# Attention's value products with the values stationary in column halves, and the mixing factors read back in 3 KB runs

## The chip, the cores and the metric

The kernel runs on one core of a Trainium2 chip. The metric is the time of one execution on the device in microseconds, taken as the median of several. TensorE multiplies (the page calls its matmuls PE and its weight loads PEld), VectorE is DVE, ScalarE is ACT, GpSimd is POOL, and SyncE is SP, which here only issues transfers.

## The reference

One layer of an encoder on 1024 tokens of width 1024. A projection `h @ w_in` feeds a dilated window attention, a gated linear attention and two merge gates; their merge, a norm and an MLP follow. What the change touches is the attention, for four head slots of width 64 and three groups g with dilations 1, 4 and 16:

```python
s = jnp.einsum('brnqhd,brnkhd->brnhqk', qb, kw) * (dh ** -0.5) + bias   # masked to the band
m = jnp.max(s, axis=-1, keepdims=True)
e = jnp.exp(s - m)
den = jnp.sum(e, axis=-1, keepdims=True)
o = jnp.einsum('brnhqk,brnkhd->brnhqd', e, vw) / den
lse = m + log(den)
```

For every token and head slot the three groups' outputs are added with weights proportional to their denominators. So with the numerators num_g = e @ v, the output is the sum over g of f_g num_g, where f_g = exp(m_g - max m) / sum over g of (exp(m_g - max m) den_g): three groups times four heads are twelve factors f for a token.

## The kernel before, in words

**Stage.** The large projections go through `mm3` (L100 to L103), three matmuls of 512 columns in a split float format for each product. They are cut in steps, and attention is cut in 24 tiles of 128 queries, groups 2, 1 and 0 in that order, eight tiles t0 to t7 each. `visit(i)` (one for each of 27 places among the steps) runs the parts of up to four tiles, so that attention's instructions fall between dense matmuls. A scheduler then fixes the order of each engine's instructions when the program is built; on the chip each engine runs its list in order and waits on semaphores.

**A tile.** `load` fetches q and k (POOL queue). `scores` (L803) multiplies in row halves, two heads at a time; VectorE adds the bias and takes the minimum (L809), ScalarE the exponential with its sum (L814); minima and sums lie in `sm`. `turned` transposes e on TensorE (L830) and copies it out as `et` (L837). `values` (L844) multiplies with `et` stationary, 128 by 128, and the 64 columns of a head's values moving, into `av` with the queries on the partitions. Each matmul in plain float shows as two records.

**Mixing.** For groups 2 and 1 numerators and `sm` are copied together into `st` (L854, L855) and stored as rows of 264 floats in `rows` (POOL queue). For group 0 a tile reads back 128 rows of each other group into R (L821), `weigh` (L881 to L884) and `blend` (L889 to L898) form the factors with queries on partitions, multiply the numerators by them and add. Two transposes on TensorE (L872), a copy (L873) and a store by POOL (L874) put the result in `yadr`, head dimension on partitions.

**After it.** `branches` (L963) loads `ygdr` (the other mixer) and `yadr` in pieces of 128x512 through SP into `pre`; ScalarE and VectorE split each in two parts, `yg` and `ya` (L148, L149). The merge multiplies them (`ps<-yg`, `ps<-ya`) and needs gates loaded from `spill` (`gate<-spill`, L1004); the tiles of the gates lie in memory that attention used.

Of the kernel before, what the change touches and what calls it, by code (L numbers as in the profile page):

```python
# [7 lines left out]
F32 = mybir.dt.float32  # L8
# [3 lines left out]
AF = mybir.ActivationFunctionType  # L12
OP = mybir.AluOpType
# [4 lines left out]
S = 1024  # L18
# [9 lines left out]
ORD = (1, 4, 8)  # L28
# [43 lines left out]
def build(tc, io):  # L72
    nc = tc.nc
    V, G, A, T, SP = nc.vector, nc.gpsimd, nc.scalar, nc.tensor, nc.sync
    P = Pools(tc)
    issued = {}
# [7 lines left out]
    avp = P.open("av", bufs=1, space=PSUM)  # L84
    dr = P.open("dram", space=DRAM)

    def load_w(src, shape, raw=None):
        if raw is None:
            raw = wp.tile(shape, F32, tag="raw", bufs=2, name="raw")
            issued["raw"] = SP.dma_start(raw, src)  # L90
        hi = wp.tile(shape, F32R, tag="whi", bufs=4, name="whi")
        A.copy(hi, raw)
        lo = wp.tile(shape, F32R, tag="wlo", bufs=4, name="wlo")
        V.tensor_tensor(lo, raw, hi.bitcast(F32), op=OP.subtract)  # L94
        return hi, lo
# [14 lines left out]
    ygdr = dr.tile([4, 128, S], F32, name="ygdr")  # L110
    sdr = dr.tile([2, 5, 128, 2, 512], F32, name="sdr")
    yadr = dr.tile([2, 128, S], F32, name="yadr")
    rows = dr.tile([2, S, 264], F32, name="rows")
    tdr = dr.tile([12, 128, 512], F32, name="tdr")
    trow = dr.tile([12, 512], F32, name="trow")
    vdr = dr.tile([S, 768], F32, name="vdr")
# [67 lines left out]
    for k in range(KT):  # L184
        n = {0: 1, 1: 1, 2: 2, 4: 2, 6: 2}.get(k)
# [18 lines left out]
    ident = cp.tile([128, 128], F32, name="ident")  # L204
# [12 lines left out]
    tp = trp.tile([128, 512], F32, tag="tr", name="tr")  # L217
# [491 lines left out]
    p0, p1 = projs[:2]  # L709
# [7 lines left out]
    a, b = p0["steps"][1], p0["steps"][4]  # L717
# [15 lines left out]
    ap_ = P.open("att", reuse_waits="tile")  # L733
# [11 lines left out]
    kq_t, kk_t, kv_t = (ring(ap_, [128, 2, n], F32, m, nm) for nm, n, m in (("aq", 128, 3), ("ak", 256, 2), ("av", 256, 3)))  # L745
    e_t, et_t = (ring(ap_, [128, 2, 256], F32, m, nm) for nm, m in (("e", 4), ("et", 3)))
    sm_t, f_t = ring(ap_, [128, 8], F32, 3, "sm"), ring(ap_, [128, 5, 4], F32, 2, "f")
    st_t, R_t = ring(ap_, [128, 264], F32, 2, "st"), ring(ap_, [128, 3, 264], F32, 2, "R")
    sc_t = turns([scp.tile([128, 2, 256], F32, tag="sc", name="sc") for _ in range(2)], 2)
    tr_t = turns([trp.tile([128, 2, 256], F32, tag="tr", name="tr") for _ in range(2)], 2)  # L750
    av = avp.tile([128, 256], F32, tag="av", name="avp")
    yat = ap_.tile([128, 2, 128], F32, name="yat")

    def window(g, t):

        if g == 2:
            return 128, 128, t * 128
        if g == 1:
            return (192, 256)[t % 2], (128, 0)[t % 2], t // 2 * 256
        return 192 if t in (0, 7) else 256, 128 if t == 0 else 64, min(max(128 * t - 64, 0), 832)  # L760

    def att(g, t):

        w, b0, k0 = window(g, t)
        b = {}
# [49 lines left out]
                                                 accum_out=sm[:, 4 + h:5 + h])  # L815

        def turned():
            if g == 0:
                b["R"] = R_t()
                for i in range(2):  # L820
                    G.dma_start(b["R"][:, 1 + i], rows[i, t * 128:t * 128 + 128])  # L821
            b["et"] = []
            nb = len(b["blks"])
            for i in range(2):
                tp, et = (x.rearrange("p a (b n) -> p a b n", n=128) for x in (tr_t(), et_t()))
                b["et"].append(et)
                for pr in range(2):
                    for j, (lo, hi, vv, p0) in enumerate(b["blks"]):
                        with tc.issue_after(issued["small"].ins):
                            T.transpose(tp[0:hi - lo, pr, j], b["e"][i][:, pr, lo:hi], ident)  # L830
                cpy = A.copy if i else V.tensor_copy
                if w == 192 and t < 7:
                    j = 0 if g == 0 else 1
                    cpy(et[0:64, :, j], tp[0:64, :, j])
                    cpy(et[:, :, 1 - j], tp[:, :, 1 - j])
                else:
                    cpy(et[:, :, 0:nb], tp[:, :, 0:nb])  # L837

        def values():
            nb = len(b["blks"])  # L840

            def part(j, h):
                lo, hi, vv, p0 = b["blks"][j]
                return T.matmul(av[:, h * 64:h * 64 + 64], b["et"][h % 2][p0:p0 + vv.shape[0], h // 2, j],  # L844
                                vv[:, h * 64:h * 64 + 64], start=j == h == 0, stop=j == nb - 1,
                                skip_group_check=True)

            with tc.issue_after(part(0, 0).ins):
                for j in range(nb):
                    for h in range(4):  # L850
                        if j or h:
                            issued["small"] = part(j, h)
            st = b["R"][:, 0] if g == 0 else st_t()
            V.tensor_copy(st[:, 0:256], av)  # L854
            V.tensor_copy(st[:, 256:264], b["sm"])  # L855
            if g == 1:
                G.dma_start(rows[0].rearrange("(u j c) w -> c u j w", u=2, c=4)[t // 2, t % 2], st)
            elif g == 2:
                G.dma_start(rows[1].rearrange("(j r) w -> r j w", r=8)[t], st)
            else:  # L860
                b["f"] = weigh(b["R"])

        def mix():
            if g == 0:
                b["o"] = o = st_t()[:, 0:256]
                blend(b["R"], b["f"], o)

        def mixed():
            if g == 0:
                tp = tr_t()  # L870
                for pr in range(2):
                    T.transpose(tp[:, pr, 0:128], b["o"][:, pr * 128:pr * 128 + 128], ident)  # L872
                A.copy(yat, tp[:, :, 0:128])  # L873
                G.dma_start(yadr[:, :, t * 128:t * 128 + 128].rearrange("b p n -> p b n"), yat)  # L874

        return load, scores, turned, values, mixed, mix

    def weigh(R):
        nm = R[:, :, 256:260]
        f = f_t()  # L880
        V.tensor_tensor(f[:, 3], nm[:, 0], nm[:, 1], op=OP.min)  # L881
        V.tensor_tensor(f[:, 3], f[:, 3], nm[:, 2], op=OP.min)
        V.tensor_tensor(f[:, 0:3], f[:, 3:4].to_broadcast([128, 3, 4]), nm, op=OP.subtract)
        A.activation(f[:, 0:3], f[:, 0:3], AF.Exp)  # L884
        return f

    def blend(R, f, o):
        den = R[:, :, 260:264]
        V.tensor_tensor(den, den, f[:, 0:3], op=OP.mult)  # L889
        V.tensor_tensor(f[:, 4], den[:, 0], den[:, 1], op=OP.add)  # L890
        V.tensor_tensor(f[:, 4], f[:, 4], den[:, 2], op=OP.add)
        V.reciprocal(f[:, 4], f[:, 4])
        V.tensor_tensor(f[:, 0:3], f[:, 0:3], f[:, 4:5].to_broadcast([128, 3, 4]), op=OP.mult)
        for g in range(3):
            num = R[:, g, 0:256].rearrange("p (h d) -> p h d", h=4)
            V.tensor_tensor(num, num, f[:, g].unsqueeze(2).to_broadcast([128, 4, 64]), op=OP.mult)
        V.tensor_tensor(R[:, 0, 0:256], R[:, 0, 0:256], R[:, 1, 0:256], op=OP.add)
        V.tensor_tensor(o, R[:, 0, 0:256], R[:, 2, 0:256], op=OP.add)  # L898

    def flat(t):  # L900
        return t.rearrange("p a b -> p (a b)")[:, 0:512]


    gated = ap_.tile([128, 3, 512], F32, tag="strip1", name="gated")
    gating = (turns([flat(e_t()) for _ in range(4)] + [flat(R_t()) for _ in range(2)], 6),
              turns([flat(et_t()) for _ in range(3)] + [gated[:, i] for i in range(3)], 6),
              turns([flat(kv_t()) for _ in range(3)], 3))

    def silu(h, hf):
# [15 lines left out]
        return load, do  # L925

    tiles = [att(g, t) for g in (2, 1, 0) for t in range(8)]

    issued["small"] = issued["pe"]

    def visit(i):

        for n, part in ((i + 1, 0), (i - 2, 3), (i, 1), (i - 1, 2), (i - 2, 5), (i - 3, 4)):
            if 0 <= n < 24:
                tiles[n][part]()


    n0 = len(steps) + 14
    for p in projs[2:]:
        steps += p["steps"]  # L940
    n1 = len(steps) - 7
    units = {}
    for i in range(27):
        units.setdefault(n0 + 1 + i * (n1 - n0) // 27, []).append(lambda i=i: visit(i))
    for i in range(8):

        n = n0 - 18 + i * 3 // 2
# [103 lines left out]
    w = []  # L1051
# [96 lines left out]
    w = [load_w(io["wo"][1, k2], [128, 2, 512]) for k2 in range(4)]  # L1148
# [241 lines left out]
    p0, p1 = pairs[:2]  # L1390
# [87 lines left out]
    R = {}  # L1478
# [326 lines left out]
```

## Time and profile before

| | |
|---|---|
| median of 3 runs | 1380.35 us (1380.32 to 1381.3) |
| the profiled execution | 1383.76 us |
| its span, and TensorE's granted clock | 1382.0 us, 0.997 |
| TensorE busy | 1370.8 us, 99% |
| VectorE, ScalarE, POOL busy | 73%, 46%, 7% |
| attention's tiles on TensorE | from 306 to 574 us |
| values, L844 | 320 records |

The span is what the profiler saw between the first and the last instruction; the execution's own time is 1.76 us longer. A row of the timeline gives start, duration, engine, line, operation, output<-inputs and shapes, and a count where like rows follow one another. Matmuls are pipelined and the end of each is modelled, so the cost of one is read from start to start of its neighbours.

### The profile page before, as it was taken

The numbers are of one execution on the slowest core, as the hardware profiler recorded it, in microseconds if no ns is written. First come the engines' busy times: TensorE is split into PE (matmuls) and PEld (weight loads), VectorE is DVE, ScalarE is ACT, GpSimd is POOL, SyncE is SP. The second block draws the span as 40 slices with busy tenths as digits, with TensorE's granted clock in tenths as the row PEclk, the third lists the DMA queues.
The fourth block names the chain that finished last, engine by engine and source line by source line (L and its number), as shares of the span: only waits on it lengthen the run. The fifth ranks groups of instructions, "written<-read, shape, count | busy, mean of one in ns | idle before, by whom it ended". The sixth has DMA issues, their size and how long they took to land.

```text
span 1382.0 us, 19028 instructions
## 1 busy us (share of the span) xinstructions
PE 1370.8 (99%) x6837; PEld 1153.0 (83%) x6837; DVE 1011.3 (73%) x1748; ACT 630.7 (46%) x1207; POOL 99.1 (7%) x153
## 2 busy tenths in 40 slices
PE   9999999999999999999999999999999999999998
PEld 6989998788888888888888888888888888888886
DVE  6377768677565677666667787878867897786988
ACT  5346645334344344354416655555556433333343
POOL 0000100013222232000001000000000000000002
PEclk9999999999999999999999999999999999999998
DMA  7262326575444443465753565666655965445313
GB/s 247 71 190 87 108 71 225 183 206 176 157 145 159 136 143 127 139 225 191 270 213 141 200 221 191 222 208 217 219 205 157 365 220 167 152 131 160 105 31 122
DMA packets 105907, 238.57 MB, mean 173 GB/s; under 512 B 20101, under 2 KB 28805, under 8 KB 105812
## 3 DMA queue, kind: packets, MB, share of 16 engines
q1 hardware_dynamic: 99220, 218.47, 47.4%
q0 software_dynamic: 6304, 18.49, 4.4%
q8 instruction: 54, 0.88, 0.3%
q10 hardware_dynamic: 288, 0.39, 0.1%
q14 instruction: 41, 0.34, 0.1%
HBM read 160.67 MB, written 77.68 MB: 172 GB/s over the span
## 4 chain that ended last, share of the span: by engine, by line
PE 90%; DVE 3%; DMA 2%; issue 2%; ACT 2%; POOL 0%; SPq 0%; POOLq 0%; ACTq 0%; DVEq 0%
PE ps L101 18%; PE ps L102 18%; PE ps L103 18%; PE mm L101 9%; PE mm L102 9%; PE mm L103 9%; PE avp L844 2%; PE tr L830 1%; PE sc L803 1%; ACT xr L1196 1%; DMA xrh<-in_xT 1%; DMA praw<-in_wfm 1%; PE sc L406 0%; PE tr L376 0%; DMA pwhi<-in_wfm 0%
## 5 line engine op out<-in xcount | busy, mean ns | idle before, releaser
L1177 ACT CAST T<-hp 128x1024 fp32r<-128x1024 f32 x36 | 37.8, 1051 | 107.6 <-PE ps L102 68.1
L102 PE MATMUL mm<-wlo,x 128*128 128x272 f32 (+1 forms) x240 | 74.5, 311 | 0.7 <-DVE wlo L94 0.7
L101 PE MATMUL mm<-whi,x 128*128 128x272 f32 (+1 forms) x240 | 75.0, 313 | 0.0
L103 PE MATMUL mm<-whi,x 128*128 128x272 f32 (+1 forms) x240 | 74.6, 311 | 0.0
L814 ACT ACTIVATE e<-e,sm 128x256 f32<-128x256 f32 (+2 forms) x96 | 43.4, 453 | 51.6 <-DVE sm L809 51.6
L102 PE MATMUL ps<-B,B 128*128 128x512 f32 x160 | 62.2, 389 | 0.0
L103 PE MATMUL ps<-B,B 128*128 128x512 f32 x160 | 62.2, 389 | 0.0
L101 PE MATMUL ps<-B,B 128*128 128x512 f32 x160 | 60.9, 390 | 0.5 <-ACT B L1177 0.5
L101 PE MATMUL ps<-T,T 128*128 128x512 f32 x144 | 56.0, 389 | 0.0
L102 PE MATMUL ps<-B,T 128*128 128x512 f32 x144 | 56.0, 389 | 0.0
L102 PE MATMUL ps<-T,T 128*128 128x512 f32 x144 | 56.0, 389 | 0.0
L103 PE MATMUL ps<-B,T 128*128 128x512 f32 x144 | 56.0, 389 | 0.0
L103 PE MATMUL ps<-T,T 128*128 128x512 f32 x144 | 56.0, 389 | 0.0
L101 PE MATMUL ps<-B,T 128*128 128x512 f32 x144 | 56.0, 389 | 0.0
L1578 DVE TENSOR_TENSOR acc<-ps,acc 128x512 f32<-128x512 f32 x68 | 45.8, 690 | 12.8 <-PE ps L103 12.2
L1178 DVE TENSOR_TENSOR T<-hp,T 128x1024 fp32r<-128x1024 f32 x36 | 44.1, 1224 | 14.1 <-ACT T L1177 14.0
L101 PE MATMUL mm<-x,pwlo 128*128 128x512 f32 x128 | 51.1, 399 | 1.4 <-DVE cu L642 1.4
L642 DVE TENSOR_TENSOR cr<-cu,mm 128x512 f32<-128x512 f32 x44 | 35.2, 800 | 23.3 <-PE mm L103 23.0
L1683 POOL TENSOR_TENSOR mv<-mv,mhalf 128x1 f32<-128x1 f32 x8 | 7.0, 880 | 607.3 <-DVE mv L1682 605.8
L103 PE MATMUL mm<-x,pwlo 128*128 128x512 f32 x128 | 50.0, 391 | 0.0
L102 PE MATMUL mm<-x,pwlo 128*128 128x512 f32 x128 | 50.0, 391 | 0.0
L101 PE MATMUL ps<-T,fraw 128*128 128x512 f32 x128 | 49.6, 390 | 0.4 <-ACT T L1177 0.4
(497 smaller groups left out, 4228.8 us busy)
## 6 DMA issues: line engine op xcount, KB each, us to landing
hdr<-c SPq DMA_DIRECT2D x112, 256.0 KB, 2.5
hp<-hdr SPq DMA_DIRECT2D x56, 512.0 KB, 3.6
spill<-cr SPq DMA_DIRECT2D x64, 256.0 KB, 3.0
praw<-in_wfm SPq DMA_DIRECT2D x16, 512.0 KB, 5.0
pwhi<-in_wfm SPq DMA_DIRECT2D x16, 512.0 KB, 4.6
gate<-spill SPq DMA_DIRECT2D x32, 256.0 KB, 3.7
wa<-in_w SPq DMA_DIRECT2D x16, 512.0 KB, 4.5
wb<-in_w SPq DMA_DIRECT2D x16, 512.0 KB, 6.4
```

Source lines behind the costliest of these rows:

```text
L101: T.matmul(ps, lh, rh, start=first and i == 0, stop=False, skip_group_check=more)
L102: T.matmul(ps, lh, rl, start=False, stop=False, skip_group_check=more)
L103: issued["pe"] = T.matmul(ps, ll, rh, start=False, stop=last and i == n - 1, skip_group_check=more)
L642: issued["add"] = V.tensor_tensor(o, a, b, op=OP.add)
L803: mm = T.matmul(sps[i][:, pr, 0:w], q[ps_, pr], k[ps_, pr, 0:w], start=True, stop=True)
L814: issued["exp"] = A.activation(e, e, AF.Exp, bias=sm[:, h:h + 1], scale=-1.0, accum_out=sm[:, 4 + h:5 + h])
L830: T.transpose(tp[0:hi - lo, pr, j], b["e"][i][:, pr, lo:hi], ident)
L844: return T.matmul(av[:, h * 64:h * 64 + 64], b["et"][h % 2][p0:p0 + vv.shape[0], h // 2, j], vv[:, h * 64:h * 64 + 64], start=j == h == 0, ...
L1177: A.copy(o[:, 0], src)
L1178: V.tensor_tensor(o[:, 1], src, o[:, 0].bitcast(F32), op=OP.subtract)
L1196: A.activation(q[i][:, k], tp[:, k], AF.Identity, bias=cols[:, c + 8:c + 9], scale=cols[:, c:c + 1])
L1578: V.tensor_tensor(m, p, m, op=OP.add)
```

## The change

**Values.** They are now the stationary operand, 64 columns wide, and `et` moves with 128 columns. Heads of even and odd number go to the left and the right half of the array's columns; the output has the head dimension on the partitions (two heads in one column of 128) and the queries as columns, as `yadr` wants it. The transposes of L872 and their copies go.

**Stores.** For groups 2 and 1 numerators go to `numdr` and `sm` alone to `smdr`, both by POOL. `quarter` reads the numerators back for two tiles at a time, by four SP transfers in runs of 256 and 128 B; `stats` reads the sums of all tiles, by POOL, into `s12`.

**Factors.** For group 0 they are formed right behind the scores (`weigh`) and a step later (`shares`), turned from 128x12 to 12x128 by TensorE (`spread`, L901), copied to `fT` by ScalarE, stored in `fdr` by ScalarE's queue, and read back by SP (`loadw`, L909): each half of the partitions gets one run of 3 KB, the same for each partition. This W has the shape of the numerators, so that four kinds of products and two sums on VectorE (L859 to L868) do the mixing, straight into what POOL stores in `yadr`. There is one W and one R.

The core of the diff (left out: the tiles' declarations in DRAM, the removed blend, the removed transposes):

```diff
+    R, W = ap_.tile([128, 2, 2, 256], F32, name="R"), ap_.tile([128, 3, 2, 128], F32, name="W")
+    st_t = turns([R[:, 1, i].rearrange("p (b n) -> p b n", b=2) for i in range(2)], 2)
...
-                return T.matmul(av[:, h * 64:h * 64 + 64], b["et"][h % 2][p0:p0 + vv.shape[0], h // 2, j],
-                                vv[:, h * 64:h * 64 + 64], start=j == h == 0, stop=j == nb - 1,
+                return T.matmul(av[64 * i:64 * i + 64, pr], vv[:, h * 64:h * 64 + 64],
+                                b["et"][i][p0:p0 + vv.shape[0], pr, j], start=j == pr == 0, stop=j == nb - 1,
                                 skip_group_check=True)
...
+            if g:
+                st = st_t()
+                V.tensor_copy(st, av[:, 0:2])
+                G.dma_start(numdr[g - 1, :, :, t * 128:t * 128 + 128].rearrange("b p n -> p b n"), st)
+                return
+            o = V.tensor_tensor(W[:, 0], av[:, 0:2], W[:, 0], op=OP.mult)
+            for i in range(2):
+                c = ORD[i + 1]
+                n = 128 // c
+                num = R[:, i].rearrange("p b (c j) -> p b j c", c=c)[:, :, t % 2 * n:t % 2 * n + n]
+                wn = W[:, i + 1].rearrange("p b (j c) -> p b j c", c=c)
+                for pr in range(2):
+                    with tc.issue_after(o.ins):
+                        o = V.tensor_tensor(wn[:, pr], num[:, pr], wn[:, pr], op=OP.mult)
+                V.tensor_tensor(mixed if i else W[:, 0], W[:, 0], W[:, i + 1], op=OP.add)
+            G.dma_start(yadr[:, :, t * 128:t * 128 + 128].rearrange("b p n -> p b n"), mixed)
...
+        def spread():
             if g == 0:
+                with tc.issue_after(issued["pe"].ins):
+                    issued["small"] = T.transpose(av[0:12, 2], b["f"][:, 0:3].rearrange("p g h -> p (g h)"), ident)
+                A.copy(fT, av[0:12, 2])
+                A.dma_start(fdr[t].rearrange("i r n -> r i n"), fT)
+
+        def loadw():
+            if g == 0:
+                for i in range(2):
+                    one = fdr[t, i:i + 1].rearrange("i r n -> i (r n)")
+                    SP.dma_start(W[64 * i:64 * i + 64].rearrange("p g b n -> p (g b n)"), one.to_broadcast([64, 768]))
...
+    def quarter(n):
+        u, q = n // 2, n % 2
+        for g in (1, 2):
+            c = ORD[g]
+            for pr in range(2):
+                src = numdr[g - 1, pr].rearrange("p (c u q j) -> p u q c j", c=c, u=2, q=2)[:, u, q]
+                dst = R[:, g - 1, pr].rearrange("p (c j) -> p c j", c=c)
+                SP.dma_start(dst, src)
...
-        for n, part in ((i + 1, 0), (i - 2, 3), (i, 1), (i - 1, 2), (i - 2, 5), (i - 3, 4)):
+        for n, part in ((i + 1, 0), (i - 1, 6), (i - 2, 3), (i, 1), (i - 1, 2)):
...
+    for i in range(26):
+        n = n0 + 1 + i * (n1 - n0) // 27
+        units.setdefault(n, []).append(lambda i=i: visit(i))
+        for k, part, later in ((i, 4, 1), (i, 5, 2), (i - 1, 7, 1)):
+            if 0 <= k < 24 and (later == 1 or k > 15):
+                units.setdefault(n + later, []).append(lambda k=k, part=part: tiles[k][part]())
+        if i in (17, 19, 21, 23):
+            units[n + 1].append(lambda i=i: quarter((i - 17) // 2))
```

The order moves where attention ends. On TensorE before, at the last attention work (the numbers behind names are buffers; L101 to L103 are dense matmuls):

```order
L844 MATMUL avp<-av_2253,et_2260 128x64
L872 MATMUL tr<-ident,st_2266 128x128 x2
L101 MATMUL mm<-x_91,pwlo 128x512
...
L103 MATMUL mm<-x_89,pwlo 128x512
L872 MATMUL tr<-ident,st_2267 128x128 x2
L101 MATMUL mm<-x_89,pwlo 128x512
```

And of the change, from the last dense matmul to the first merge products (`et_2262` with `av_2254` is t6, `av_2255` t7):

```order
L103 MATMUL mm<-x_94,px 128x512
L901 MATMUL avp<-ident,f_2267 12x128
L845 MATMUL avp<-et_2262,av_2254 64x128
...
L845 MATMUL avp<-et_2260,av_2254 64x128
L830 MATMUL tr<-ident,e_2258 128x128 x4
L830 MATMUL tr<-ident,e_2259 128x128 x4
L845 MATMUL avp<-et_2261,av_2255 64x128
...
L101 MATMUL ps_5184<-yg_5003,whi 128x512
...
L101 MATMUL ps_5181<-ya_5000,whi 128x512
```

Before, 117 dense matmuls lie between the last L872 and the first `ps<-ya`, and 27 between the two pairs of transposes. Now the values of t6 and t7 stand behind all dense matmuls, and `ps` products follow at once; the last row, the first that needs the second half of `ya` (that of t4 to t7), is the sixteenth of them.

On SP before, where the loads for the merge are issued:

```order
L963 DMA pre<-ygdr 128x512 x4
L963 DMA pre<-yadr 128x512
L621 DMA spill<-cr_2106 128x512
L963 DMA pre<-yadr 128x512
L621 DMA spill<-cr_2107 128x512
L621 DMA spill<-cr_2108 128x512
L963 DMA pre<-yadr 128x512 x2
```

And of the change:

```order
L925 DMA R<-numdr 128x4x64 x2
L925 DMA R<-numdr 128x8x32 x2
L909 DMA W<-fdr 64x768 x2
L623 DMA spill<-cr_2110 128x512
L1039 DMA gate<-spill 128x512 x8
L909 DMA W<-fdr 64x768 x2
L1039 DMA gate<-spill 128x512
L998 DMA pre<-ygdr 128x512 x4
L998 DMA pre<-yadr 128x512 x4
```

The loads for the merge were spread between the spills of the last projections, and the gates followed them. Now the last quarter of R and the W of t6 come behind nearly all spills, eight gates stand between the W of t6 and that of t7, and all loads for the merge stand behind that.

More of the change, by code (lines that the diff above doesn't have):

```diff
@@ L112, in build @@
     yadr = dr.tile([2, 128, S], F32, name="yadr")
-    rows = dr.tile([2, S, 264], F32, name="rows")
+    numdr = dr.tile([2, 2, 128, S], F32, name="numdr")
+    smdr = dr.tile([2, S, 8], F32, name="smdr")
+    fdr = dr.tile([8, 2, 6, 128], F32, name="fdr")
     tdr = dr.tile([12, 128, 512], F32, name="tdr")
@@ L747, in build @@
     sm_t, f_t = ring(ap_, [128, 8], F32, 3, "sm"), ring(ap_, [128, 5, 4], F32, 2, "f")
-    st_t, R_t = ring(ap_, [128, 264], F32, 2, "st"), ring(ap_, [128, 3, 264], F32, 2, "R")
+    R, W = ap_.tile([128, 2, 2, 256], F32, name="R"), ap_.tile([128, 3, 2, 128], F32, name="W")
+    s12, fT = ap_.tile([128, 8, 2, 8], F32, name="s12"), ap_.tile([12, 128], F32, name="fT")
+    st_t = turns([R[:, 1, i].rearrange("p (b n) -> p b n", b=2) for i in range(2)], 2)
     sc_t = turns([scp.tile([128, 2, 256], F32, tag="sc", name="sc") for _ in range(2)], 2)
     tr_t = turns([trp.tile([128, 2, 256], F32, tag="tr", name="tr") for _ in range(2)], 2)
-    av = avp.tile([128, 256], F32, tag="av", name="avp")
-    yat = ap_.tile([128, 2, 128], F32, name="yat")
+    av = avp.tile([128, 3, 128], F32, tag="av", name="avp")
+    mixed = ap_.tile([128, 2, 128], F32, name="mixed")
     def window(g, t):
@@ L817, in turned @@
         def turned():
[L818 to L821, printed above, removed]
             b["et"] = []
@@ L842, in part @@
             def part(j, h):
+                i, pr = h % 2, h // 2
                 lo, hi, vv, p0 = b["blks"][j]
-                return T.matmul(av[:, h * 64:h * 64 + 64], b["et"][h % 2][p0:p0 + vv.shape[0], h // 2, j],
-                                vv[:, h * 64:h * 64 + 64], start=j == h == 0, stop=j == nb - 1,
+                return T.matmul(av[64 * i:64 * i + 64, pr], vv[:, h * 64:h * 64 + 64],
+                                b["et"][i][p0:p0 + vv.shape[0], pr, j], start=j == pr == 0, stop=j == nb - 1,
                                 skip_group_check=True)
@@ L852, in values @@
                             issued["small"] = part(j, h)
-            st = b["R"][:, 0] if g == 0 else st_t()
-            V.tensor_copy(st[:, 0:256], av)
-            V.tensor_copy(st[:, 256:264], b["sm"])
+            if g:
[4 more added lines that the diff above has]
+            o = V.tensor_tensor(W[:, 0], av[:, 0:2], W[:, 0], op=OP.mult)
@@ L856, in values, with weigh @@
+            G.dma_start(yadr[:, :, t * 128:t * 128 + 128].rearrange("b p n -> p b n"), mixed)
+        def weigh():
+            sm = b["sm"]
             if g == 1:
-                G.dma_start(rows[0].rearrange("(u j c) w -> c u j w", u=2, c=4)[t // 2, t % 2], st)
+                G.dma_start(smdr[0].rearrange("(u j c) w -> c u j w", u=2, c=4)[t // 2, t % 2], sm)
             elif g == 2:
-                G.dma_start(rows[1].rearrange("(j r) w -> r j w", r=8)[t], st)
+                G.dma_start(smdr[1].rearrange("(j r) w -> r j w", r=8)[t], sm)
@@ L860, in values @@
             else:
-                b["f"] = weigh(b["R"])
-        def mix():
-            if g == 0:
-                b["o"] = o = st_t()[:, 0:256]
-                blend(b["R"], b["f"], o)
-        def mixed():
-            if g == 0:
[L870 to L898, printed above, removed]
+                o = s12[:, t]
@@ new lines, in weigh, with shares @@
+                b["f"] = f = f_t()
+                V.tensor_tensor(f[:, 3], sm[:, 0:4], o[:, 0, 0:4], op=OP.min)
+                V.tensor_tensor(f[:, 3], f[:, 3], o[:, 1, 0:4], op=OP.min)
+                V.tensor_tensor(f[:, 0], f[:, 3], sm[:, 0:4], op=OP.subtract)
+                V.tensor_tensor(f[:, 1:3], f[:, 3:4].to_broadcast([128, 2, 4]), o[:, :, 0:4], op=OP.subtract)
+                A.activation(f[:, 0:3], f[:, 0:3], AF.Exp)
+        def shares():
+            if g == 0:
+                f, den, o = b["f"], b["sm"][:, 4:8], s12[:, t, :, 4:8]
+                with tc.issue_after(issued["add"].ins):
+                    V.tensor_tensor(den, den, f[:, 0], op=OP.mult)
+                with tc.issue_after(issued["add"].ins):
+                    V.tensor_tensor(o, o, f[:, 1:3], op=OP.mult)
+                V.tensor_tensor(f[:, 4], den, o[:, 0], op=OP.add)
+                V.tensor_tensor(f[:, 4], f[:, 4], o[:, 1], op=OP.add)
+                V.reciprocal(f[:, 4], f[:, 4])
+                V.tensor_tensor(f[:, 0:3], f[:, 0:3], f[:, 4:5].to_broadcast([128, 3, 4]), op=OP.mult)
@@ new lines, in att, with stats @@
+        return load, scores, turned, values, weigh, shares, spread, loadw
+    def stats(g):
+        for u in range(2):
+            G.dma_start(s12[:, 4 * u:4 * u + 4, g - 1],
+                        smdr[g - 1, 512 * u:512 * u + 512].rearrange("(t p) w -> p t w", p=128))
+    def quarter(n):
[6 more added lines that the diff above has]
+                SP.dma_start(dst, src)
@@ L904, in build @@
     gated = ap_.tile([128, 3, 512], F32, tag="strip1", name="gated")
-    gating = (turns([flat(e_t()) for _ in range(4)] + [flat(R_t()) for _ in range(2)], 6),
+    gating = (turns([flat(e_t()) for _ in range(4)] + [R[:, i].rearrange("p b n -> p (b n)") for i in range(2)], 6),
               turns([flat(et_t()) for _ in range(3)] + [gated[:, i] for i in range(3)], 6),
@@ L931, in visit @@
     def visit(i):
-        for n, part in ((i + 1, 0), (i - 2, 3), (i, 1), (i - 1, 2), (i - 2, 5), (i - 3, 4)):
+        for n, part in ((i + 1, 0), (i - 1, 6), (i - 2, 3), (i, 1), (i - 1, 2)):
             if 0 <= n < 24:
                 tiles[n][part]()
+        if i in (12, 16):
+            stats(2 if i == 12 else 1)
     n0 = len(steps) + 14
@@ L942, in build @@
     units = {}
-    for i in range(27):
-        units.setdefault(n0 + 1 + i * (n1 - n0) // 27, []).append(lambda i=i: visit(i))
+    for i in range(26):
[6 more added lines that the diff above has]
+            units[n + 1].append(lambda i=i: quarter((i - 17) // 2))
     for i in range(8):
```

## The prediction

> **What bounds the kernel now.** The page first: its span, its busy times and the chain that ended last.
>
> ```profile
> span 1382.0 us, 19028 instructions
> PE 1370.8 (99%) x6837; PEld 1153.0 (83%) x6837; DVE 1011.3 (73%) x1748; ACT 630.7 (46%) x1207; POOL 99.1 (7%) x153
> PE 90%; DVE 3%; DMA 2%; issue 2%; ACT 2%; POOL 0%; SPq 0%; POOLq 0%; ACTq 0%; DVEq 0%
> ```
>
> TensorE is busy 99% of the span and holds 90% of the chain. Then the windows over the stage that the change touches (columns: window, its length, then busy us of PE, PEld, DVE, ACT and POOL, granted clock, DMA share).
>
> ```profile
> 300.00:400.00 100.00, 100.00 (x552) 82.99 (x551) 62.82 (x184) 44.22 (x136) 29.12 (x44) 1.00 0.50 156
> 400.00:500.00 100.00, 100.00 (x577) 84.06 (x576) 63.99 (x188) 39.20 (x111) 26.00 (x39) 1.00 0.44 137
> 500.00:580.00 80.00, 79.15 (x436) 66.41 (x436) 55.19 (x166) 30.21 (x84) 16.01 (x25) 1.00 0.43 141
> 580.00:600.00 20.00, 20.00 (x89) 16.44 (x88) 16.29 (x25) 11.20 (x19) 0.00 (x0) 1.00 0.63 201
> ```
>
> From 300 to 600 us TensorE leaves 0.85 us empty. Every attention tile is threaded between matmuls of the dense projections, so its softmax and transfers cost nothing, and only its TensorE time counts. That cover must last until the merge reads attention's output, so I looked at the end of the stage on the timeline: the last transposes of a mixed tile, the last loads and casts of that output, and its first consumer.
>
> ```profile
> 573.86 0.38 PE L872 MATMUL tr<-ident,st 128*128 128x128 f32 x2
> 585.85 0.92 SPq L963 DMA_DIRECT2D pre<-yadr  x2
> 592.27 1.14 ACT L148 CAST ya<-pre 128x512 fp32r<-128x512 f32 x2
> 599.80 0.39 PE L103 MATMUL mm<-x,px 128*128 128x512 f32 x1
> 600.71 0.39 PE L101 MATMUL ps<-ya,whi 128*128 128x512 f32 x1
> ```
>
> Attention is done on TensorE at 574; its output is cast by about 593.4 and wanted at 600.71, 7 us later. In between stand 117 dense matmuls; from 599.80 to 600.71 four take 0.91 us, 0.2275 each, so the cover is 26.6 us.
>
> **What leaves TensorE and what comes.** The values' product today:
>
> ```profile
> 446.30 0.39 PE L103 MATMUL mm<-x,pwlo 128*128 128x512 f32 x1
> 446.52 1.89 PE L844 MATMUL avp<-av,et 128*128 128x64 f32 x16
> 448.35 1.13 PE L803 MATMUL sc<-ak,aq 64*128 64x256 f32 x8
> L844 PE MATMUL avp<-av,et x320: 217/275/323, 318.0 to 567.2; 128*128 128x64 f32 x136, 64*128 64x64 f32 x24
> ```
>
> Sixteen records take 1.83 us, start to start; 320 of them make 20 such sets, 36.6 us. No product here uses column halves. The nearest row is the use of row halves with 128 columns moving, as the new product moves 128:
>
> ```profile
> 81.05 1.16 PE L406 MATMUL sc<-q,k 64*128 64x128 f32 x16
> 82.14 0.50 PE L101 MATMUL mm<-x,whi 128*128 128x512 f32 x1
> ```
>
> Sixteen records take 1.09 us with the way in: two run at once. With 0.06 us for the way out I take 1.15 per set, 23.0 in all: **-13.6**. The end on the good side is 16 at half of 0.114 with nothing at the borders, 0.91, so -18.3; on the bad side halves that take turns, 1.83 and a border each time, +2 to +3. A border between array shapes is seen here:
>
> ```profile
> 25.26 0.39 PE L102 MATMUL sc<-x,whi 128*128 128x512 f32 x1
> 25.58 1.03 PE L218 MATMUL tr<-oh,rb 99*12 99x512 f32 x2
> 26.54 0.50 PE L103 MATMUL mm<-x,wlo 128*128 128x512 f32 x1
> ```
>
> 0.32 us instead of 0.2275 on the way in, 0.09 more, and 0.11 by the 0.50 against 0.39 on the way out. The Trainium skill, TensorEngine Tiling (Array Packing), Key Properties, speaks against the change here: a change of tiling mode drains the array, though tiles load and multiply independently. The trace agrees in size: some 0.2 us for a visit there and back, so 24 visits would pay 4.8 by it, of which the 1.15 above has about half, and the sum would stand 2 us higher.
>
> The transposes at L872 go, and eight of the factors come (L901). A transpose costs what the rows of a late visit show; they also give the softmax its times:
>
> ```profile
> 545.27 0.92 PE L803 MATMUL sc<-ak,aq 64*128 64x192 f32 x8
> 546.13 1.09 PE L830 MATMUL tr<-ident,e 128*128 128x128 f32 x8
> 546.98 0.47 PE L103 MATMUL mm<-xT,pwhi 128*128 128x512 f32 x1
> 547.11 0.35 DVE L809 CUSTOM_DVE_ANT_0 e<-sc,strip 128x192 f32<-128x192 f32 x1
> 548.55 0.08 DVE L809 DVE_READ_ACCUMULATOR2_ANT sm<- 128x1 f32 x1
> 549.66 0.19 ACT L814 ACTIVATION_READ_ACCUMULATOR e<-e,sm 128x1 f32 x1
> ```
>
> Eight take 0.85, 0.106 each: 16 out, **-1.7**; 8 in, **+0.9** (with a border each up to +2.5). TensorE's work falls by 14.4 us (bounds -19.1 and +3).
>
> VectorE, ScalarE and POOL have about 36, 56 and 71 us of every 100 free while dense work runs; what comes there (the products by W, eight copies fT, the split stores of sums and numerators, four loads of s12) costs nothing as long as it does. ScalarE issues eight stores of fT, and behind each wait its copies of et. The SP queue now carries 16 loads of R and 16 of W; behind them wait spills and weight loads, and the DMA engines are 0.43 to 0.50 busy there. All of that loses its cover only at the end.
>
> **The new end.** In the order of the changed program the values of the last two tiles (t6, t7) stand behind the last dense matmul, and only 15 products of the merge come before one that needs their result. From the scores of t7 on, the path is (S = their start):
>
> ```profile
> 544.83 0.17 DVE L893 TENSOR_TENSOR f<-f 128x12 f32<-128x12 f32 x1
> 546.32 0.42 DVE L854 COPY R<-avp 128x256 f32<-128x256 f32 x1
> ```
>
> - Dense work ends at 0.85 + 0.85 + 12 x 0.2275 = S+4.4.
> - VectorE first multiplies t5: 256-element operations at 0.42, 128-element ones at 0.29 (no row; the middle of 0.17 and 0.42): 3 x 0.42 + 4 x 0.29 = 2.4. Four minima follow (547.11 to 548.63, 1.5), the exponentials end 1.2 later, then some seven small operations of 0.17: the factors' transpose starts at about S+6.4. TensorE has waited 2.0.
> - The values of t6 take until S+7.5. They also need R and W. R's last quarter is issued from S+1.8, and is cut in 3072 runs of 128 and 256 B.
>
> ```profile
> DMA packets 3347, 1.45 MB, mean 290 GB/s; under 512 B 3119, under 2 KB 3119, under 8 KB 3347
> q1 hardware_dynamic: 3347, 1.45, 107.6%
> ```
>
> In that window (275 to 280 us) a packet took 1.076 x 5 x 16 / 3347 us = 25.7 ns of one of 16 engines, so 3072 take 4.9 us. With about 2 to the first byte (vdr<-stgv below) R has landed at S+8.7, and W behind it at S+9.0. The Trainium skill, DMA: Bandwidth & Descriptors, Specifications, gives 512 B as the least size for line rate. The trace agrees only in part: that window, nearly all runs under 512 B, moved 290 GB/s. [...]
>
> ```profile
> vdr<-stgv SPq DMA_DIRECT2D x16, 192.0 KB, 1.9
> R<-rows POOLq DMA_DIRECT2D x16, 132.0 KB, 2.5
> gate<-spill SPq DMA_DIRECT2D x32, 256.0 KB, 3.7
> gate<-spill SPq DMA_DIRECT2D x14, 256.0 KB, 4.9
> yadr<-yat POOLq DMA_DIRECT2D x8, 128.0 KB, 3.1
> pre<-yadr SPq DMA_DIRECT2D x4, 256.0 KB, 3.1
> ```
>
> - Products of t6 to S+11.4. Only then is the one W free: two loads, 0.3 and 3.1 (between R<-rows and gate<-spill), S+14.8; products of t7, S+17.2; yadr 3.1, S+20.3; pre<-yadr 0.3 + 3.1, S+23.7; a cast of 0.6: S+24.3.
> - So 19.9 us after the last dense matmul, with TensorE work of 0.1 + 1.15 + 0.85 + 1.15 + 15 x 0.2275 = 6.7 inside: **+13.2** idle.
> - Eight gate loads of 256 KB stand ahead of W(t7) on SP: between nothing and the 1.2 from 3.7 to 4.9; I take **+0.6**.
>
> TensorE then stands for stretches of 2, 2, about 5 and 3 us. What the clock does after little work:
>
> ```profile
> 1371.66 1.88 PE L1700 MATMUL ps<-c,ones 1*128 1x512 f32 x5
> 1374.00:1376.00 2.00, 1.88 (x4) 0.38 (x2) 1.97 (x6) 0.67 (x2) 0.62 (x1) 0.72 0.00 0
> 1376.00:1382.00 6.00, 1.22 (x2) 0.50 (x2) 0.84 (x2) 1.17 (x3) 0.00 (x0) 0.50 0.49 176
> ```
>
> One-row matmuls from 1371.66, and from about 1374.9 on half the clock: some 3.2 us of little work are enough. The 5 us stretch should do that; the 15 products after it are covered by the next wait, and of the merge behind that a part of 3 us runs at half, 0 to +2.5; I take **+0.8**. The Trainium skill, TensorE: Matmul & The Clock Gate, What's actually happening, has the same as a window of about 3.4 us for both directions; by it the price would be up to 1.7, one window at half.
>
> **Sum.** -14.4 + 13.2 + 0.6 + 0.8 = +0.2 us. The profiled execution took 1383.76 (span 1382.0 and 1.76 around it), 3.4 above the median of 1380.35; against the median that is **1380.5**, no change. What this measurement can tell apart is 0.2%, 2.8 us.
>
> **Rivals.**
> - *The end is short* (1371). R's runs land with the rest (1.5 less at t6), W lands in R<-rows' 2.5 (0.6), yadr in vdr<-stgv's 1.9 (1.2), gates and clock cost nothing (1.4), and halves with cheap borders give -18.3 (4.7): 9.4 less. For it: the short transfers exist, and DMA engines are under half busy. Against: the SP queue is at its fullest just there.
> - *The end is long* (1387), slower. It decides once more than 17 us of idle stand behind the last dense matmul. Gates, W, five pre<-ygdr and the yadr loads share one queue: eight times 256 KB at 290 GB/s are 7.2 us, so W(t7) may land 3.5 later, R and W of t6 1 later, and the clock costs 2.5, not 0.8: +6.2. For it: the 4.9 of gate<-spill in a burst. Against: half of those gates can go out early, since only later ones wait for t7's transposes.
> - *Column halves take turns* (1396), slower: nothing of 13.6 is won and 2 is paid for borders, +15.6. For it: no record of this form exists here. Against: row halves do run at once.
> - *The change doesn't do what it says*: the order shows the new products in place and 16 transposes gone, so I give this nothing.
>
> **Chances.** Forecast 0.42 (its own range 1376 to 1385), short end 0.25, long end 0.23, halves that take turns 0.10. Of the forecast's share 0.32 lies within 0.2%, and of the rivals' a little (0.05); so faster 0.28, same 0.37, slower 0.35. The range: 1373 leaves some of the short end out, 1392 the halves that take turns.
>
> **What would show it.** Sets of 16 values' records at 1.1 to 1.2 us, pairs starting together; L872 gone. PE busy about 14 us less, and about as much idle between the last `mm` and the products of `ya`: waits for f, for W twice, for pre<-ygdr and pre<-yadr, in this order. Window clock of 0.5 to 0.9 in the 5 us behind. Wrong, if sets cost over 1.5, if idle there is under 9 or over 17, or if idle appears while dense work still runs.

## The result

| | median, us | runs |
|---|---|---|
| before | 1381.3 | 5 (1380.32 to 1382.94) |
| changed | 1386.39 | 5 (1384.3 to 1387.98) |
| ratio | 1.0035 | 95% interval 1.0020 to 1.0049 |

The change makes the kernel 0.35% slower, 5 us. The forecast was no change (1380.5, between 1373 and 1392); the measured time is near that of the rival called the long end (1387).

The page of the changed kernel, span, busy times and chain:

```profile
span 1384.4 us, 19088 instructions
PE 1363.3 (98%) x6829; PEld 1132.7 (82%) x6829; DVE 1008.7 (73%) x1748; ACT 629.8 (45%) x1207; POOL 105.1 (8%) x157
PE 93%; DVE 3%; ACT 2%; DMA 1%; issue 0%; SPq 0%; DVEq 0%; ACTq 0%
```

TensorE is busy 7.5 us less than the 1370.8 of before and the span is 2.4 longer. The spans differ by less than the medians because the profiled execution of the kernel before was a long one (1383.76): its stage of attention and merge begins at 265.1 us, and that of the change at 262.4. The windows show where it stands empty (columns as in the prediction: busy us of PE, PEld, DVE, ACT, POOL, then the granted clock, the DMA share and GB/s):

```profile
400.00:500.00 100.00, 100.00 (x563) 78.95 (x562) 61.96 (x174) 40.55 (x114) 25.68 (x37) 1.00 0.50 156
500.00:560.00 60.00, 58.77 (x316) 46.87 (x315) 40.46 (x118) 22.50 (x58) 7.98 (x11) 1.00 0.54 151
584.00:588.00 4.00, 2.94 (x21) 2.41 (x22) 0.64 (x5) 0.26 (x1) 0.00 (x0) 0.61 0.93 283
588.00:592.00 4.00, 2.06 (x22) 1.41 (x20) 2.83 (x8) 3.12 (x5) 0.72 (x1) 0.93 0.98 329
592.00:596.00 4.00, 0.00 (x0) 0.00 (x0) 0.00 (x0) 3.20 (x6) 0.00 (x1) 0.50 0.92 261
596.00:600.00 4.00, 0.25 (x1) 0.25 (x1) 2.21 (x7) 1.42 (x4) 0.00 (x0) 0.50 1.01 324
600.00:604.00 4.00, 4.00 (x9) 2.83 (x10) 3.12 (x6) 2.27 (x4) 0.73 (x1) 0.50 0.27 94
604.00:608.00 4.00, 3.96 (x15) 2.82 (x15) 1.38 (x2) 1.74 (x3) 0.00 (x0) 0.83 0.91 271
```

Until 580 us little is lost (1.2 us). From 584 to 605 TensorE is for the most part empty or at half clock, and until 600 the DMA engines are over 0.9 busy. TensorE's own rows of that end, from the timeline:

```profile
578.04 0.92 PE L807 MATMUL sc<-ak,aq 64*128 64x192 f32 x8
584.72 0.28 PE L901 MATMUL avp<-ident,f 128*12 128x128 f32 x1 [1.96 <-DVE f L896]
585.35 1.98 PE L845 MATMUL avp<-et,av 128*64 128x128 f32 x16 [0.34 <-ACT fT L902]
587.25 1.56 PE L830 MATMUL tr<-ident,e 128*128 128x128 f32 x8
590.13 1.24 PE L845 MATMUL avp<-et,av 128*64 128x128 f32 x16 [1.31 <-DVE et L837]
599.75 0.79 PE L101 MATMUL ps<-yg,whi 128*128 128x512 f32 x1 [8.38 <-ACT yg L150]
```

The waits add up to 12.0 us, and most of what runs between them and just behind runs at half speed: the values of t6 take 1.9 us, and the first merge product 0.69 to the next. The values of t7 fall in a stretch at full clock.

**A ledger of the stage.** In both traces I added the distances from each matmul's start to the next, from the first `mm<-xT,pwlo` to the first `ps<-wo`. The stage took 400.85 us before and 405.85 now. Up to the start of the last dense matmul it is 15.4 shorter (335.35 to 319.93), from there on 20.4 longer (65.51 to 85.91). Of the latter 3.2 us are work that has only moved there (two sets of values, a set of transposes, one of factors). So **12.2 us were won and 17.2 lost**: 12.0 of waiting and about 5 of half clock.

### The profile page after: what moved, and what is told of

Read it like the earlier page. It is cut to its first block, busy times and chain, and to the rows that moved or that the text cites. A ratio compares the mean times of both kernels' runs of the same rounds, so it can differ in the third digit from the quotient of the medians.

```text
span 1384.4 us, 19088 instructions
## 1 busy us (share of the span) xinstructions
PE 1363.3 (98%) x6829; PEld 1132.7 (82%) x6829; DVE 1008.7 (73%) x1748; ACT 629.8 (45%) x1207; POOL 105.1 (8%) x157
## 4 chain that ended last, share of the span: by engine, by line
PE 93%; DVE 3%; ACT 2%; DMA 1%; issue 0%; SPq 0%; DVEq 0%; ACTq 0%
PE ps L101 18%; PE ps L103 18%; PE ps L102 18%; PE mm L101 10%; PE mm L102 10%; PE mm L103 10%; PE avp L845 1%; PE sc L807 1%; PE tr L830 1%; ACT xr L1231 1%; DMA pre<-ygdr 0%; DMA xr<-in_xT 0%; PE sc L408 0%; PE tr L378 0%; DMA fdr<-fT 0%
## 5 line engine op out<-in xcount | busy, mean ns | idle before, releaser
L101 PE MATMUL mm<-whi,x 128*128 128x272 f32 (+1 forms) x240 | 75.0, 313 | 0.0
L103 PE MATMUL mm<-whi,x 128*128 128x272 f32 (+1 forms) x240 | 74.7, 311 | 0.0
L103 PE MATMUL ps<-B,B 128*128 128x512 f32 x160 | 62.2, 389 | 0.0
L101 PE MATMUL ps<-B,B 128*128 128x512 f32 x160 | 60.9, 390 | 0.5 <-ACT B L1212 0.5
L101 PE MATMUL ps<-T,T 128*128 128x512 f32 x144 | 56.0, 389 | 0.0
L103 PE MATMUL ps<-T,T 128*128 128x512 f32 x144 | 56.0, 389 | 0.0
L101 PE MATMUL ps<-B,T 128*128 128x512 f32 x144 | 56.0, 389 | 0.0
L103 PE MATMUL ps<-B,T 128*128 128x512 f32 x144 | 56.0, 389 | 0.0
L1718 POOL TENSOR_TENSOR mv<-mv,mhalf 128x1 f32<-128x1 f32 x8 | 7.0, 881 | 607.3 <-DVE mv L1717 605.8
L101 PE MATMUL mm<-x,pwlo 128*128 128x512 f32 x128 | 50.5, 395 | 0.0
L103 PE MATMUL mm<-x,pwlo 128*128 128x512 f32 x128 | 50.2, 392 | 0.0
L101 PE MATMUL ps<-T,fraw 128*128 128x512 f32 x128 | 49.6, 390 | 0.4 <-ACT T L1212 0.4
```

The source lines that it names most:

```text
L101: T.matmul(ps, lh, rh, start=first and i == 0, stop=False, skip_group_check=more)
L103: issued["pe"] = T.matmul(ps, ll, rh, start=False, stop=last and i == n - 1, skip_group_check=more)
```

## Experiments

Times are medians, and each ratio is to the kernel before on the same chip. The medians of the kernel before lie between 1380.74 and 1381.64 there, so two variants that differ by 1 to 2 us are compared by their ratios and by the length of the stage in their traces (the ledger).

### The values alone

```diff
-                return T.matmul(av[:, h * 64:h * 64 + 64], b["et"][h % 2][p0:p0 + vv.shape[0], h // 2, j],
-                                vv[:, h * 64:h * 64 + 64], start=j == h == 0, ...
+                return T.matmul(av[64 * i:64 * i + 64, pr * 128:pr * 128 + 128], vv[:, h * 64:h * 64 + 64],
+                                b["et"][i][p0:p0 + vv.shape[0], pr, j], start=j == pr == 0, ...
```

> The kernel before with one part of the change: the values stationary in column halves, output in the same place of memory but turned; all that follows is the old code, so the mixed result is not attention's (it multiplies numerators in the wrong layout); every transfer and operation is as before. Theory (the gain in TensorE time is real and the end of the stage eats it): values 36.1 us to some 22.5, borders of 1.5 against, so 12 us faster, about 1369; the last attention work moves to the same place among the dense matmuls as before and no idle appears. Rival (the halves' gain is eaten inside the stage by borders and waits): 1376 or more.

Measured: 1370.64, ratio 0.9927 (0.9910 to 0.9943), 10.6 us faster. One set of values, with a dense matmul ahead, and the first product of `ya` behind the last dense one:

```profile
553.38 0.39 PE L103 MATMUL mm<-xT,pwhi 128*128 128x512 f32 x1
553.70 1.24 PE L845 MATMUL avp<-et,av 128*64 128x128 f32 x16
554.88 0.44 PE L873 MATMUL tr<-ident,st 128*128 128x128 f32 x2
...
588.07 0.39 PE L103 MATMUL mm<-x,px 128*128 128x512 f32 x1
588.29 0.39 PE L101 MATMUL ps<-ya,whi 128*128 128x512 f32 x1
```

The set takes 1.18 us where it took 1.83, and no idle follows. By the ledger the values went from 36.1 to 24.0 us, and the 1117 dense matmuls, whose distances hold the way in, from 258.8 to 261.3: 12.1 won, 2.5 paid at borders. The theory holds, 1.6 us short of its number.

### The mixing alone

```diff
-                return T.matmul(av[64 * i:64 * i + 64, pr], vv[:, h * 64:h * 64 + 64],
-                                b["et"][i][p0:p0 + vv.shape[0], pr, j], start=j == pr == 0, ...
+                return T.matmul(av[:, pr, 64 * i:64 * i + 64], b["et"][i][p0:p0 + vv.shape[0], pr, j],
+                                vv[:, h * 64:h * 64 + 64], start=j == h == 0, ...
```

> The changed kernel with the other part alone: values' products in their old form (transposed weights stationary, 128 by 128, values' 64 columns moving), their result left in the wrong layout for the mixing, so that the output is not attention's; all else as in the change. Theory (the halves are worth what they were alone, the mixing's chain loses the rest and more): values 22.5 back to 36.1 us, borders of 1.5 away, 11 to 13 slower than the change, about 1398; dense work ends that much later and the end of the stage has the same 12 us of idle. Rival (with the old values the visits are slower, more of the chain is covered): less than 6 slower, under 1392.

Measured: 1397.97, ratio 1.0123 (1.0105 to 1.0141), 17.2 slower than before. Against the change, the dense work ends 9.9 us later in the stage (the values under it cost 12.3 more, the dense matmuls 2.0 less), and the end behind it is the same (86.0 us from the last dense matmul to `ps<-wo`, 85.9 in the change). The two parts alone add to -10.6 + 17.2 = +6.6; together they gave +5.1.

### The gates' loads behind those of ya

```diff
+                if n == 7:                     # the last load of ya
+                    issued["fw"] = ld
...
-        SP.dma_start(g, spill[wi, :, hf * 512:hf * 512 + 512])
+        with tc.issue_after(issued["fw"].ins):
+            SP.dma_start(g, spill[wi, :, hf * 512:hf * 512 + 512])
```

> The changed kernel with the loads of the merge's gates tied behind the last load of ya on SP, so that no gate stands ahead of W of t7 or of the loads for the merge. Theory (the queue): W of t7 lands 3.5 to 4 us after its issue rather than 6.2, pre<-ygdr earlier by about as much, ya's last cast at about 602.5 rather than 606.6; 3 to 4 us faster than the change, about 1382.5. Rival (latencies alone make the chain, the queue is harmless): no difference, 1386.

Measured: 1383.95, ratio 1.0025 (1.0014 to 1.0036), 2.4 below the change. The intervals overlap, but the stage is shorter by as much in the trace (403.5 us instead of 405.8). First the change's rows of SP and VectorE, then those of this kernel:

```profile
584.44 6.47 SPq L1039 DMA_DIRECT2D gate<-spill  x8
591.01 1.09 SPq L909 DMA_DIRECT2D W<-fdr  x2
597.75 0.42 DVE L859 TENSOR_TENSOR W<-avp,W 128x256 f32<-128x256 f32 x1 [6.88 <-DMA W<-fdr]
```

```profile
591.21 1.09 SPq L909 DMA_DIRECT2D W<-fdr  x2
595.86 0.42 DVE L859 TENSOR_TENSOR W<-avp,W 128x256 f32<-128x256 f32 x1 [4.67 <-DMA W<-fdr]
```

The products of t7 start 6.7 us after the first issue of W with eight gates ahead of it, and 4.65 without. So the gates cost 2.1 of the 3.5 us by which W came later than I had counted. Without them it still takes 1.3 more than the 3.4 of the prediction, and that is not owed to transfers ahead of it: from 588 to 592 us this trace has a DMA share of 0.01. Over all tiles of the change W's loads landed 3.3 to 6.1 us after their issue, with a median of 4.1.

### Work in the idle stretch

```diff
+            if g == 0 and t == 7:
+                idle = mmtile()
+                for n in range(34):            # 42 in the second run
+                    with tc.issue_after(issued["small"].ins):
+                        issued["small"] = T.matmul(idle, xh(0, slice(0, 128)), xh(1, slice(0, 512)), start=True, stop=True)
```

> The changed kernel with 34 matmuls of 512 columns whose results are not used, behind the values of t7, 7.7 us of work in the idle stretch of 8.4 us. Theory 1 (the half clock behind the idle stretch costs its whole 3 us): products of the merge run at 0.2275 from the start and the kernel gains about 3 us, 1383. Theory 2 (the wait for ya's second half ends last, the slow products only fill it): granted clock 1.0 in the stretch, the products done some 3 us earlier, and an idle stretch of 3 us before the first product of the second half in their place; within 0.5 us of the change, 1386.

Measured: 1387.65, ratio 1.0047 (1.0031 to 1.0062); no gain. But it did not settle the question, since the clock fell again in the 1.0 us that was left. So a second run:

> The changed kernel with 42 such matmuls in place of 34, 9.5 us of work, which reach beyond the cast of yg. With 34 a gap of 1.0 us was left before the merge's products, and the clock fell to half in them all the same. Theory 1 (the half clock costs its whole 3 us): products of yg and of ya's first half run at 0.2275 from about 600.6, and the kernel is some 3 us faster than the change, 1383. Theory 2 (the loads of ya's second half end last): those 15 products are done at about 604, TensorE then waits some 2 us for the cast at 606, and the time stays, 1386 to 1388.

Measured: 1386.1, ratio 1.0037 (1.0021 to 1.0053), the change's time. Its windows, and the first product that needs ya's second half:

```profile
600.00:604.00 4.00, 4.00 (x19) 3.08 (x18) 2.68 (x5) 1.48 (x3) 0.73 (x1) 1.00 0.21 62
604.00:608.00 4.00, 4.00 (x18) 3.08 (x17) 1.39 (x2) 1.46 (x3) 0.00 (x0) 1.00 0.84 277
605.85 0.98 PE L101 MATMUL ps<-ya,whi 128*128 128x512 f32 x3
```

The merge runs at full clock throughout (its 288 products took 65.7 us, 68.5 in the change), and the product comes at 605.85 with its cast done at 605.8 (606.28 and 606.2 in the change). The wait of 2 us that theory 2 named did not show, because the added matmuls themselves ran slowly at first and ended at 602.2 rather than 600.6. What is shown: with the clock back, ya's second half comes hardly earlier and the time is the same (the stage too: 405.8 us in both traces). About 3 us of half clock in the change lie inside the wait for ya.

### Two buffers for W

```diff
+    Ws = [W]                                   # the second, W1, in memory of group 1's strip
...
+            W = Ws[t % 2]
```

> The changed kernel with W in two buffers and nothing else; two gates still stand ahead of t7's W on SP and seven between it and the loads for the merge. Theory (with the gates in front, the loads for the merge end last and the second W alone is worth little): at most 1 us faster than the change, 1385 to 1387. Rival (the single W is the cause of the late end by itself): as much as W's 6 us, 1381.

Measured: 1388.46, ratio 1.0053 (1.0035 to 1.0070): no gain, against the rival, and outside the theory's 1385 to 1387 on the slow side. It is 2 us above the change, though the intervals overlap. Only two gates now stand ahead of W, seven behind it, and the loads of ygdr behind all nine are issued at 594.96 instead of 592.84; TensorE waits 9.6 us for them.

With the gates behind ya as well:

> The kernel with the gates' loads behind ya, and W in two buffers by turns (the second in memory that group 1's bias strip has left), so that W of t7 need not wait for the products of t6. Theory (one W makes t7's load start only at 591): W of t7 lands before the values of t7 are done, products of t7 follow them at about 592, ya's second half is there at about 601.5 instead of 604.3; 2.5 us faster than with the gates moved alone, about 1381.5. Rival (the loads of the merge and the half clock behind them end last anyway): 1384, unchanged.

Measured: 1382.53, ratio 1.0011 (1.0001 to 1.0020): 1.4 us below the gates moved alone, where 2.5 were expected. A gain is not shown: the intervals overlap, and the stage in its trace is no shorter (404.0 us against 403.5). Its rows:

```profile
582.28 4.46 SPq L930 DMA_DIRECT2D R<-numdr  x4
590.53 1.11 SPq L914 DMA_DIRECT2D W<-fdr  x2
...
590.76 0.37 DVE L869 TENSOR_TENSOR W<-R,W 128x128 f32<-128x128 f32 x1 [1.34 <-DMA R<-numdr]
595.05 0.42 DVE L861 TENSOR_TENSOR W<-avp,W 128x256 f32<-128x256 f32 x1 [2.52 <-DMA W<-fdr]
```

W of t7 is free to be loaded from the start, but is issued at 590.53 all the same (591.21 with one W): in the trace SP waits for the store of its factors, issued at 585.81. R's runs were under way beside it until 590.76; that they held the store up is argued and not shown. So the single W was one of two waits that ended close together. R too came later here, as its loads now stand behind W of t6 on SP (issued from 582.28 instead of 580.09).

### R in whole rows

```diff
-                src = numdr[g - 1, pr].rearrange("p (c u q j) -> p u q c j", c=c, u=2, q=2)[:, u, q]
-                dst = R[:, g - 1, pr].rearrange("p (c j) -> p c j", c=c)
-                SP.dma_start(dst, src)
+                SP.dma_start(R[:, g - 1, pr], numdr[g - 1, pr, :, n * 256:n * 256 + 256])
```

> The kernel with two W and the gates' loads behind ya, and R read in whole rows of 1 KB (512 runs for a quarter where there were 3072); the columns of the other groups come in their stored order, so that the mixed output is not attention's. There the products of t6 waited until 590.8 for R's last load, issued from 582.3 to 586.7. Theory (the small runs make the last quarter late, in issue and in landing): R lands at about 587, the products of t6 end at about 589.5 rather than 592.5, ya's last cast 2 us earlier, 1380 to 1381. Rival (W's load through DRAM ends last anyway): 1382.5, unchanged.

Measured: 1383.91, ratio 1.0013 (1.0002 to 1.0023); runs from 1380.06 to 1385.52. In the trace the theory's steps are there:

```profile
581.70 1.91 SPq L927 DMA_DIRECT2D R<-numdr  x4
589.28 0.43 DVE L870 TENSOR_TENSOR mixed<-W 128x256 f32<-128x256 f32 x1
601.61 1.31 ACT L150 CAST ya<-pre 128x512 fp32r<-128x512 f32 x2 [3.31 <-DMA pre<-yadr]
```

R's four issues take 1.9 us instead of 4.5, the products of t6 end at 589.7 instead of 592.5, the first cast of ya's second half starts at 601.61 instead of 603.37 (the last ends only 0.4 earlier), and the stage is 1.8 us shorter by the ledger. The times do not show it: ratio 1.0013 against 1.0011. The granted clock differs from run to run of one kernel and moves them more: here two of ten runs had a mean clock of 0.997 and took 1380.06 and 1381.0, the other eight 0.993 to 0.994 and 1383.08 to 1385.52. Whether R's small runs cost the end anything in time stays open.

### Closer visits

```diff
-        n = n0 + 1 + i * (n1 - n0) // 27
+        n = n0 + 1 + i * (n1 - n0) // 40
```

> The changed kernel with the visits set closer (the divisor 27 of their places is 40), so that the values of t7 come 36 dense matmuls (8.2 us) before the last dense one, and nothing but t7's mixing and store is left behind. Theory (the gain is there, the uncovered end eats it): idle behind the last dense matmul falls from 12 to about 2 us, full clock, 1369 to 1372. Rival (the chain of f, W and the store slows the dense work wherever it lies, or transfers collide earlier): 1378 or more.

Measured: 1377.81, ratio 0.9978 (0.9968 to 0.9987): 3.4 faster than before and 8.6 than the change, but not the 1369 to 1372 expected: it is the time of the rival, 1378. The rival's first reason, slower dense work, is not there (its dense matmuls take 260.9 us, 260.6 in the change); late transfers are. One wait is left, and 10.2 us of half clock around its end:

```profile
583.95 0.39 PE L103 MATMUL mm<-x,px 128*128 128x512 f32 x1
591.57 1.45 PE L101 MATMUL ps<-yg,whi 128*128 128x512 f32 x2 [7.22 <-ACT yg L150]
```

The loads of ygdr stand on SP behind W of t7 and spills that dense work releases; they were issued from 584.80. With two W as well:

> The kernel with closer visits, and W in two buffers by turns. There TensorE waited 7.2 us for the loads of ygdr, issued at 584.8 behind spills that follow W of t7 on SP. Theory (these loads stand behind W of t7 and the spills that it delays on SP): with the second W they are issued at about 583, idle falls from 7.2 to about 5 us, 2 us faster than closer visits alone, about 1375.5. Rival (spills wait for dense work, whatever W does): 1378, unchanged.

Measured: **1370.52**, ratio 0.9925 (0.9907 to 0.9943), 10.2 us faster than before and 16 than the change. The output is attention's.

```profile
581.30 1.84 SPq L1003 DMA_DIRECT2D pre<-ygdr  x4
...
586.03 0.50 PE L101 MATMUL ps<-yg,whi 128*128 128x512 f32 x1 [1.42 <-ACT yg L150]
587.34 0.50 PE L101 MATMUL ps<-yg,whi 128*128 128x512 f32 x1 [0.81 <-ACT yg L150]
...
584.00:588.00 4.00, 1.77 (x7) 0.85 (x5) 2.06 (x3) 1.79 (x3) 0.00 (x0) 1.00 0.93 289
```

The loads are issued 3.5 us earlier, as fewer spills now stand ahead of them on SP, and the waits add up to 2.2 us. In this trace the granted clock stays at 1.00 behind them, which I had not counted: another 2.6 us in the merge (65.8 instead of 68.4). Does the spacing win by itself?

> The kernel before, with the visits set as close as in the two runs with closer visits (27 of their places become 40). Theory (what those runs won is the change's work, freed of its end): nothing behind the last dense matmul was uncovered in the kernel before, so closer visits move nothing: 1380.7, within 2. Rival (closer visits win by themselves, whatever the values do): 1375 or less.

Measured: 1380.83, ratio 0.9995 (0.9986 to 1.0004): no. What the two kernels above win is the change's own work, once its end is covered.

## What the prediction had right and what it had wrong

**What held.** The bound, and that only TensorE's time counts under the cover. The end behind the last dense matmul ate TensorE's gain, as forecast, and then more than that (17.2 us against 12.2). The halves run two at once: the prediction's 1.15 us for a set is 1.02 to 1.18 in the traces. The end of the dense work lay 4.6 us after the scores of t7 (4.4 predicted), the factors' transpose 6.7 (6.4), the start of the products of t6 9.9 (9.0), with R's issue at 1.3 and W behind it. The order of the waits was the one named: f, W twice, pre<-ygdr, pre<-yadr.

**TensorE's term was 2 us too good.** -14.4 was predicted, and 12.2 were won by the ledger. The values and the transposes L872 gave 13 and 1.5; the dense matmuls grew by 1.9, and 0.4 more idle stood in the cover. The step that fell short is the reading of 1.09 us as a set "with the way in". The way in stands ahead of the first record, in the distance of the dense matmul before it: 0.32 us (553.38 to 553.70 above), where it was 0.22 (446.30 to 446.52 in the prediction). The Trainium skill, TensorEngine Tiling (Array Packing), Key Properties, which makes each change of tiling mode drain the array, would have put the sum 2 us higher; the ledger agrees in size, with 1.9 in the change and 2.5 with the values alone.

**The end was mis-sized at one load.** Times from the start of t7's scores (578.04), as the prediction summed them:

| step | predicted | measured |
|---|---|---|
| values of t6 done | 7.5 | 9.2 |
| products of t6 done | 11.4 | 12.8 |
| W of t7 in use | 14.8 | 19.7 |
| products of t7 done | 17.2 | 22.1 |
| ya's second half cast | 24.3 | 28.2 |

W took 6.9 us from the end of the products, and not 3.4. I priced it between two medians from stretches in which the DMA engines were less busy (0.41 from 484 to 570 us for R<-rows, 0.70 from 600 to 700 for gate<-spill), though in the same text eight gates and R's runs stood in its queue. Here the share was over 0.9. The price that would have been right stood with the rival, "W(t7) may land 3.5 later". Moving the gates took 2.1 of it away; the rest is not explained by the queue ahead, and its cause stays open.

R's price was too high, without harm, as the products of t6 waited for W. The 25.7 ns of a packet mixed 3119 small ones with 228 large ones that moved 0.67 of the 1.45 MB; by the trace's own packets 256 B took 18 ns, and in the change 128 B took 13.6, so that 3072 runs are 2.9 us and not 4.9. The 290 GB/s of that window are no rate of small runs either: 256 B in 18 ns on each of 16 engines make some 228.

**The clock.** I took 0.8 of a possible 2.5 and it was granted at half for 3.4 us from 584.9 and for 13.7 from 591.7. Its rows lost about 5 us, 0.9 of it on the values of t6 and 3.2 on the merge. Yet that price is not to be added to the late load: with the merge at full clock the time was the same. Waiting plus half clock came to 17.2 where 14.6 stood in the sum; with TensorE's 2.2, that makes +5.0 out of +0.2.

**The choice among cases.** The long end, with a chance of 0.23 against the forecast's 0.42, had the late W right (3.5) and nearly the late start of t6's products (0.9 measured, 1 named). Its condition was more than 17 us of idle behind the last dense matmul, and that was not met: 12.0 us were idle, less than the 13.2 of the forecast, and the 17.2 above hold 5.2 of half clock. It also added 1.7 for the clock, which the work in the idle stretch showed to lie inside a wait, and left out TensorE's 2.2. That its 1387 is so near 1386.39 is in part luck. What spoke for it in the profile, the 4.9 us of gates in a burst, came from a busy stretch (DMA share 0.81 from 603.84 to 616.2 us). The reading behind the forecast was right in kind and wrong in which row stood nearest.

## What to carry to other kernels

Work that is hidden in a dense stage is free only as long as the stage lasts: look at what is issued behind the last dense matmul, and put the last pieces early enough for their whole chain of loads. Price a load by a row from a stretch in which the DMA engines are as busy as they will be there, not by the median over the kernel. Of a change that shortens the bound engine and lengthens a chain, run the halves apart: here the one was worth 10.6 us and the other cost 17.2, and with the chain covered the whole change was worth 10.2, no more than the values alone.

## What was not expected of the hardware

- **The clock falls after short waits, and not each time.** Waits of 1.96 and 0.34 us around one small transpose, from 582.8 on, were followed by a granted clock of 0.61 over 584 to 588. With 34 added matmuls at full clock, waits of 1.02 and 0.32 us around 600 were enough for 0.74 over 600 to 604. Waits of 1.42 and 0.81 in the fastest kernel left it at 1.00. So did the very same waits around the same transpose, 1.95 and 0.34, in five other kernels here, among them that with 42 added matmuls (1.00 over 584 to 588; the values of t6 took 1.0 us there, not 1.9). Inside each kernel the stretches at half lasted 3.4 us or three to five times that (3.4 and 13.7 in the change, 10.2 with closer visits, 17.1 with the mixing alone). The Trainium skill, TensorE: Matmul & The Clock Gate, What's actually happening, calls the window of activity free-running, so that it depends on where work falls in it. The runs agree that the length of a wait alone does not decide. Its table of states asks for an idle window of about 3.4 us; a window without any work was not needed here.
- **Small runs cost the issuing queue too.** Four loads of R in runs of 128 and 256 B took 2.7 to 4.5 us to issue on SP at the end of the stage, and 1.9 us in whole rows; a spill took 0.32. The busy queue counts as well: four loads of `ygdr`, in runs of 2 KB, took 1.8 to 3.5.
- **A small store takes as long as a large one.** The factors of a tile are 6 KB. From their store's issue to the load of W that needs them 4.7 us passed in the kernel with two W and the gates moved (585.81 to 590.53), and 3.7 with R in whole rows (585.54 to 589.22). The 128 KB of `yadr` landed in 3.1 before and in a median of 4.3 at the end of the change.
